# w_down by products over all rows, from block sums that are made earlier and stored

## The chip, the cores and the metric

The kernel runs on one core of one Trainium2 chip. The metric is the device time in microseconds (us) of one execution. The core has five engines that run side by side: PE (TensorE, matmuls), DVE (VectorE), ACT (ScalarE), POOL (GpSimd) and SP (SyncE, which here issues nearly all DMA transfers). Each works through its own queue in order, and an instruction waits at the head of its queue until what it needs is done.

## The reference, cut to what matters

A decoder layer in float32 for 1024 positions and a width of 1024:

```python
h = rmsnorm(x, norm_mix)
proj = h @ w_in
y_a = (g_s5 @ w_a_val) * sigmoid(g_s5 @ w_a_gate)      # g_s5 = gelu(S5 state-space mixer)
y_b = mamba2_mixer(...) @ w_b
y_c = memory_attention(...) @ w_c
x = x + (g_a * y_a + g_b * y_b + g_c * y_c) @ w_out
h = rmsnorm(x, norm_ffn)
up = causal_dwconv(h @ w_up)                           # 2 x 2816 channels, width 3
x = x + (silu(up[..., :2816]) * up[..., 2816:]) @ w_down
return rmsnorm(x, norm_final)
```

The change touches the last product (2816 rows of w_down), the places where its operands come into being, and one buffer of the S5 mixer.

## The kernel before, in words

**Matmuls in float32.** `split_into` (line 140) splits each operand into a high part (a copy on ACT into fp32r) and a low part (a subtraction on DVE, or on POOL where `e=G`). `mm3` (346) then makes three matmuls: high x high, high x low, low x high. All elementwise two-operand work goes through `tt` (125), and the recorder of line 51 stands for every instruction in the profile, so the profile names tiles rather than lines.

**Weights.** `w_raw` (240) loads weights into a ring of 3 raw buffers (`wr`), `w_ent` (261) splits them into a ring of 6 entries (`wh`, `wl`), and `take` (291) hands them out, up to 6 entries ahead of use. All loads are issued by SP.

**The tag ev.** Many short-lived tiles share a ring of 4 buffers in the pool `ep`, tag `ev`. In the S5 stage these are the outputs of the gate products (`qt`, `gt`), the loaded parameters `s5bc`, the decay `s5D0` and the temporary `s5ph` of the phases.

**The S5 stage** (`s5_work`, 773) runs as a generator beside the gate products: after every quarter of a product's matmuls (`tick`, 330) it may take a step. ACT and PE keep the program's order there. It works on four quarters of the channels. For each, `double` (896) makes 128 phases on POOL by seven doublings (`cmul`, 624, six operations each); PE transposes the input maps (`s5bps`), ACT copies them out (`s5BTr`, `s5BTi`); `lag_maps` (865) makes the lag map, to which POOL adds the diagonal (`s5w`) before it is stored in `kS` and loaded back; `scan` (924) and `back` (942) on DVE make the states `s5Hr`, `s5Hi`; `outputs` (957) multiplies them on PE (`s5yp`).

**w_a, w_b.** `gemm_fm` (354) makes 48 matmuls for one block of 128 columns over all 1024 positions. Eight pairs of products of w_a (gate, value) are followed by 16 of w_b. `y_norm` (1477) runs beside them: it loads the 16 blocks of y (`yq`, 2 buffers), squares them on ACT, adds them on POOL and makes the reciprocal norm. `load_chunk` (1426) loads and splits the moving operands (`ck`, `hl`) between w_a and w_b.

**w_up.** Blocks of 128 channels; the first 3 pairs (activation, gate) by plain products, the others by `wino_run` (395): seven products for a pair of blocks instead of eight, a Strassen-Winograd scheme, 84 matmuls for a pair. POOL makes the sums of the weights' blocks (`wS`). The epilogue `ff_epi` makes the convolution (`ff_conv`, two operations on DVE), the silu on ACT, and `ff_b` (1608) the gated product on DVE, which it stores in DRAM as `aS`, one row block of 128 channels at a time.

**w_down, before.** The same scheme of seven products (`PRODS`, 219) for out = A B, with A the activations and B = w_down, cut in half by rows (blocks k and k + 11), by positions and by columns. It runs over three chunks of 4, 4 and 3 row blocks (`CUT`, 221): for each chunk all seven products, P1, P2, P6, P5, P7, P3, P4. `d_load` (1656) loads whole rows of 512 KB for a chunk; `d_prep` (1673) splits the operands of one entry (a product's block of rows), and, at the entries of P2, P6 and P5, makes the sums S1 to S4 (DVE) and T1 to T4 (POOL) in place. Some splits are given to POOL. An entry feeds 12 matmuls; 77 entries in all. After each product and chunk `done` (1774) adds the accumulators `dP` into the rows `x1f` (first by an ACT copy); the residual rows are loaded from `x1S` and added on POOL during the second chunk. `half_done` (1734) and `final_norm` (1741) make the last norm: blocks 0 to 3 after the last P3, blocks 4 to 7 at the end of the last P4, whose 3 entries are run block by block.

The first four entries are prepared before the epilogue of the last pair of w_up (`ff_last`), in the order in which ACT must take them. From `SY.on = True` (1717) on, SP issues transfers in the program's order.

Of the kernel before, what the change touches and what calls it, by code (L numbers as in the profile page):

```python
# [58 lines left out]
def hybrid_layer(ctx: ExitStack, tc: tile.TileContext, a: dict, out: bass.AP):  # L59
# [161 lines left out]
    CUT, NK = [0, 4, 8, 11], NFF // 2  # L221
    NC = len(CUT) - 1
    D_POOL = {"S1", "S2", "S3", "S4"}
    prods = [(p, c) for c in range(NC) for p in ("P1", "P2", "P6", "P5", "P7", "P3", "P4")]
    dents = [(p, c, k) for p, c in prods for k in range(CUT[c], CUT[c + 1])]
# [392 lines left out]
    aS = dram("aS", [DFF, T])  # L618
# [858 lines left out]
    def y_norm():  # L1477

        acc = wbp.tile([P, T], F32, name="acc")
        for i in range(16):  # L1480
            yq = wbp.tile([P, T], F32, tag="yq", name="yq", bufs=2)
            SY.dma_start(out=yq, in_=ySSD[i * P:(i + 1) * P, :])
            S.activation(out=acc if i == 0 else yq, in_=yq, func=AF.Square)
            if i:
                tt(acc, acc, yq, ALU.add, G)
            yield
        sst = ps.tile([P, 8], F32, tag="s", name="sst")
        for i in range(8):
            TE.matmul(sst[:, i:i + 1], acc[:, i * P:(i + 1) * P], ones[:, 0:1], start=True, stop=True)
        ivt = wbp.tile([P, 8], F32, name="ivt")  # L1490
        rsqrt(ivt, sst, 8, 1.0 / 2048, cp)
        yield
        for hf in range(2):
            ib = ps.tile([P, 4, P], F32, tag="s", name="ib")
            for i in range(4):
                dgi = wbp.tile([P, P], F32, tag="dgi", name="dgi", bufs=4)
# [29 lines left out]
    for pr in range(2):  # L1526
# [62 lines left out]
    ff = ExitStack()  # L1589
    t3p = ff.enter_context(pool("t3p", side="right"))  # L1590
# [16 lines left out]

    def ff_b(j, va, ob):
        vb = ff_conv(NFF + j, ob)
        tt(va, va, vb, ALU.mult)  # L1610
        SY.dma_start(out=aS[j * P:(j + 1) * P, :], in_=va)

    def ff_epi(n, ua, ub):
        ff_b(FF_PLAIN + n, ff_a(FF_PLAIN + n, ua), ub)
# [31 lines left out]

    set_banks("5", 0, 8)
    dap = ctx.enter_context(pool("da"))
    dps = [ctx.enter_context(pool(nm, side="right")) for nm in ("dw1", "dw2", "da1", "da2")]
    dxp = ctx.enter_context(pool("dx", side="right"))  # L1650
    xfp = ctx.enter_context(pool("xf", side="right"))
    lo, hi = slice(0, HALF), slice(HALF, T)
    blk, dready = {}, deque()
    dpos = {"ent": 0, "use": 0}

    def d_load(k, b, halves=False):

        kk = k + NK * b
        rw = dps[b].tile([P, T], F32, tag="r", name=f"rw{b}", bufs=4)
        ra = dps[2 + b].tile([P, T], F32, tag="r", name=f"ra{b}", bufs=4)  # L1660
        names = (("A12", "A22"), ("B21", "B22")) if b else (("A11", "A21"), ("B11", "B12"))
        srcs = (aS[kk * P:(kk + 1) * P, :], a["w_down"][0][kk * P:(kk + 1) * P, :])
        parts = []
        for t, nms, src in zip((ra, rw), names, srcs):
            for s, nm in zip((lo, hi), nms):
                blk[nm, k] = t[:, s]
            if halves:
                parts.append([(t[:, s], src[:, s]) for s in (lo, hi)])
            else:
                SY.dma_start(out=t, in_=src)  # L1670
        return parts

    def d_prep():

        p, c, k = dents[dpos["ent"]]
        dpos["ent"] += 1
        an, wn_ = PRODS[p]
        r = []
        for nm, pl, tg, bufs in ((an, dap, "a", RING), (wn_, wp, "w", RING)):
            h = pl.tile([P, HALF], F32R, tag=tg + "h", name=tg + "h", bufs=bufs)  # L1680
            l = pl.tile([P, HALF], F32R, tag=tg + "l", name=tg + "l", bufs=bufs)
# [4 lines left out]
        def new(s, nm):  # L1686
            blk[nm, k] = dxp.tile([P, HALF], F32, tag=s, name=s, bufs=4)
            return blk[nm, k]

        def inplace(nm, old, i0, i1, e=V):  # L1690
            o = blk[old, k]
            tt(o, blk[i0, k], blk[i1, k], ALU.subtract, e)
            blk[nm, k] = o

        if p == "P2":
            tt(new("xa", "S1"), blk["A21", k], blk["A22", k], ALU.add)
            tt(new("xw", "T1"), blk["B12", k], blk["B11", k], ALU.subtract, G)
            inplace("S3", "A21", "A11", "A21")
            inplace("S2", "A11", "S1", "A11")
            inplace("T2", "B11", "B22", "T1", G)  # L1700
            inplace("S4", "A12", "A12", "S2")
        elif p == "P6":
            inplace("T3", "B12", "B22", "B12", G)
        elif p == "P5":
            inplace("T4", "B21", "B21", "T2", G)
        elif p in ("P7", "P4") and c + 1 < NC:
            kn = k - CUT[c] + CUT[c + 1]
            if kn < CUT[c + 2]:
                d_load(kn, int(p == "P4"))
# [8 lines left out]
    first = [(d_load(k, 0, True), d_load(k, 1, True)) for k in range(CUT[1])]
    for parts in [f[0] for f in first] + [f[1] for f in first]:
        for t in parts:  # L1720
            SY.dma_start(out=t[0][0], in_=t[0][1])
# [35 lines left out]
    FIRST = {("P1", 0), ("P6", 0), ("P5", 0), ("P7", 0)}  # L1757
    acc4 = [None, None]
    TE.on = True
    for p, c in prods:  # L1760
        n = CUT[c + 1] - CUT[c]
        last = (p, c) == prods[-1]
        more = p in ("P6", "P7", "P3")
        tg = (prods.index((p, c))) % 2
        if not more:
            acc4[tg] = [ps2[tg].tile([P, HALF], F32, tag="s", name=f"d{p}") for _ in range(4)]
        bank = acc4[tg]

        def part(i, k, r):
            ah, al, bh, bl = r  # L1770
            mm3(bank[i], [(ah[:, i * P:(i + 1) * P], al[:, i * P:(i + 1) * P], bh, bl)],
                first=k == 0 and not more, last=k == n - 1, again=more)

        def done(i):
            for q, (i0, s) in enumerate(DST[p]):
                xc = x1[i0 + i][:, s]
                if (p, c) in FIRST and q == 0:
                    copy(xc, bank[i])
                else:
                    tt(xc, xc, bank[i], ALU.add)  # L1780
# [11 lines left out]
        for k in range(n):  # L1792
            r = d_take()
            for i in range(4):
                part(i, k, r)
        for i in range(4):
            done(i)
        if c == 1 and p in ("P1", "P6", "P7", "P4"):
            for i in range(2):
                i += 2 * ("P1", "P6", "P7", "P4").index(p)  # L1800
                xr = ep.tile([P, D], F32, tag="ev", name="x1r", bufs=4)
                SY.dma_start(out=xr, in_=x1S[i * P:(i + 1) * P, :])
                tt(x1[i], x1[i], xr, ALU.add, G)
        if c == NC - 1:
            for i in range(4):
                if p in ("P2", "P7", "P3"):
                    half_done(i + 4 * (p == "P7"), lo if p == "P2" else hi)
            if p == "P3":
                final_norm(0, 4)
# [25 lines left out]
```

## Time and profile before

| | us |
|---|---|
| median of 3 runs | 2365.66 (2365.19 to 2370.77) |
| the profiled execution, its own time | 2366.27 |
| its span from the first to the last instruction | 2364.6 |
| PE, busy (modelled) | 2215.3 (94%) |
| PE, weight loads | 1833.3 (78%) |
| DVE, busy | 1697.1 (72%) |
| ACT, busy | 987.4 (42%) |
| POOL, busy | 912.3 (39%) |
| stage of S5 beside the gates, about | 522 to 800 |
| w_a and w_b | 1218 to 1562 |
| w_up | 1671 to 2098 |
| w_down and the last norm | 2098 to 2364.6 |

Matmuls overlap, so a matmul of 389 ns is followed by the next after less than that; the pace is read from the distance of starts. In a group of instructions, "idle before" is the time the engine stood idle just before them, with what ended it. A wait names whose event ended it, not necessarily the cause behind that.

### The profile page before, as it was taken

How to read it: one execution, taken by the hardware profiler on the slowest of the kernel's cores; microseconds unless marked ns; L12 is line 12 of the kernel's file. 1: busy time of each engine (PE TensorE's matmuls, PEld its weight loads, DVE VectorE, ACT ScalarE, POOL GpSimd, SP SyncE). 2: the span in 40 equal slices, each digit the busy share in tenths (PEclk: the TensorE clock that was granted, in tenths of full speed). 3: DMA queues.
4: the chain of work that ended last, by engine and by line, in shares of the span. 5: the costliest groups of instructions: out<-in, count | busy, mean ns of one | idle time of the engine just before them, and what ended most of it. 6: DMA issues, size and time to landing. Idle time of an engine off the chain costs nothing. (4 is left out here: it accounts for less than half of the span.)

```text
span 2364.6 us, 30701 instructions
## 1 busy us (share of the span) xinstructions
PE 2215.3 (94%) x11239; PEld 1833.3 (78%) x11239; DVE 1697.1 (72%) x2320; ACT 987.4 (42%) x1762; POOL 912.3 (39%) x691
## 2 busy tenths in 40 slices
PE   6999999998878999999989999999999999987996
PEld 5777888887667788777768888899788888876775
DVE  7899877876556576989463264534977787878998
ACT  4435545542222366565351132122355455444434
POOL 4422433426566005888140002200323333353775
PEclk9999999999999999999999999999999999998998
DMA  4323434465344447997762254432122222243231
GB/s 146 108 81 98 125 107 125 125 147 106 74 94 102 126 131 247 301 293 256 250 230 71 73 169 135 132 116 90 63 80 83 87 81 81 72 175 125 82 118 71
DMA packets 339191, 305.95 MB, mean 129 GB/s; under 512 B 31969, under 2 KB 297057, under 8 KB 339041
## 3 DMA queue, kind: packets, MB, share of 16 engines
q1 hardware_dynamic: 337888, 299.80, 41.3%
q10 hardware_dynamic: 1152, 4.19, 0.4%
q8 instruction: 88, 1.44, 0.2%
q14 instruction: 63, 0.51, 0.1%
HBM read 226.61 MB, written 77.33 MB: 129 GB/s over the span
## 5 line engine op out<-in xcount | busy, mean ns | idle before, releaser
L51 DVE TENSOR_TENSOR wl<-wr,wh 128x512 fp32r<-128x512 f32 (+1 forms) x275 | 223.6, 824 | 170.2 <-ACT wh L51 163.9
L51 ACT ACTIVATE wh<-wr 128x512 fp32r<-128x512 f32 (+1 forms) x305 | 186.6, 625 | 374.5 <-PE g L51 224.6
L51 PE MATMUL g<-hlH,wh 128*128 128x512 f32 x736 | 288.8, 394 | 8.6 <-DVE fv L51 4.6
L51 PE MATMUL g<-hlL,wh 128*128 128x512 f32 x736 | 289.7, 394 | 5.5 <-DVE hlL L51 5.5
L51 PE MATMUL g<-hlH,wl 128*128 128x512 f32 x736 | 288.2, 392 | 0.0
L51 POOL TENSOR_TENSOR wS<-wr 128x512 f32<-128x512 f32 x82 | 128.2, 1563 | 346.5 <-DMA wr<-in_w_in 155.7
L51 PE MATMUL gh<-hlH,wh 128*128 128x512 f32 (+1 forms) x464 | 193.7, 418 | 0.0
L51 PE MATMUL gh<-hlH,wl 128*128 128x512 f32 (+1 forms) x464 | 183.0, 394 | 0.0
L51 PE MATMUL gh<-hlL,wh 128*128 128x512 f32 (+1 forms) x464 | 182.8, 394 | 0.0
L51 DVE TENSOR_TENSOR wl<-wS,wh 128x512 fp32r<-128x512 f32 x164 | 129.8, 793 | 70.4 <-ACT wh L51 70.3
L51 PEld LDWEIGHTS g<-hlH,wh 128*128 128x128 f32 x736 | 139.4, 189 | 39.3 <-issue 5.4
L51 PEld LDWEIGHTS g<-hlL,wh 128*128 128x128 f32 x736 | 139.2, 189 | 38.6 <-DVE hlL L51 10.4
L51 ACT ACTIVATE wh<-wS 128x512 fp32r<-128x512 f32 x164 | 102.4, 628 | 148.4 <-PE wA L51 90.5
L51 PEld LDWEIGHTS g<-hlH,wl 128*128 128x128 f32 x736 | 139.2, 189 | 28.4
L51 POOL TENSOR_TENSOR wS<-wr,wS 128x512 f32<-128x512 f32 x41 | 94.8, 2313 | 153.7 <-DVE wl L51 143.8
L51 POOL TENSOR_TENSOR mg<-mg,gi 128x1024 f32<-128x1024 f32 x15 | 41.8, 2784 | 275.5 <-DVE gi L51 275.5
L51 PE MATMUL dP<-wh,ah 128*128 128x512 f32 x308 | 122.6, 398 | 14.9 <-ACT ah L51 9.0
L51 PE MATMUL dP<-wl,ah 128*128 128x512 f32 x308 | 122.6, 398 | 12.6 <-DVE wl L51 12.6
L51 PE MATMUL dP<-wh,al 128*128 128x512 f32 x308 | 121.9, 396 | 1.8 <-POOL al L51 1.8
L51 PEld LDWEIGHTS gh<-hlH,wh 128*128 128x128 f32 (+1 forms) x464 | 87.4, 188 | 24.2 <-issue 5.4
L51 PEld LDWEIGHTS gh<-hlL,wh 128*128 128x128 f32 (+1 forms) x464 | 87.3, 188 | 21.8 <-issue 3.6
L51 PEld LDWEIGHTS gh<-hlH,wl 128*128 128x128 f32 (+1 forms) x464 | 86.9, 187 | 20.8
(389 smaller groups left out, 6078.3 us busy)
## 6 DMA issues: line engine op xcount, KB each, us to landing
wr<-in_w_in SPq DMA_DIRECT2D x76, 512.0 KB, 3.7
wr<-in_w_up SPq DMA_DIRECT2D x44, 512.0 KB, 3.7
xc<-xcS SPq DMA_DIRECT2D x32, 640.0 KB, 5.8
seg<-aD SPq DMA_DIRECT2D x32, 512.0 KB, 7.0
gi<-gS SPq DMA_DIRECT2D x32, 512.0 KB, 3.8
xcS<-xv SPq DMA_DIRECT2D x24, 512.0 KB
gS<-gt SPq DMA_DIRECT2D x24, 512.0 KB, 4.4
aS<-fv SPq DMA_DIRECT2D x22, 512.0 KB, 2.6
```

The costliest lines, as they stand in the source:

```text
L51: r = f(*args, **kw)
```

## The change

Four things change together.

1. The row blocks are paired as 2k and 2k + 1 (not k and k + 11), and the seven products run one after the other over all 11 pairs, with no chunks.
2. All block sums are made earlier and stored in DRAM. `down_sums` makes T1 to T4 of w_down on POOL, in 22 pieces of 128 x (2 x 256), in steps beside w_a and the first eight products of w_b, and stores them in `tS`. `ff_sums` makes S1 to S4 on DVE when the second block of a pair is finished in w_up, and stores all seven operands in `aS`. For the last pair it runs within P1 of w_down.
3. In w_down, `d_raw` loads one 256 KB block of each operand per entry, 4 entries ahead of the splits; all splits are on ACT and DVE, none on POOL. x1 is loaded whole from `x1S` within P1 and every accumulator is added to it on DVE.
4. In S5, `double` takes its temporary from the stage's own pool (tag `ph`) and writes the first product of each component directly in place.

Along with this, `yq` has 1 buffer (2 before), `dgi` 2 (4 before), and the steps of `y_norm` are taken one per product.

The diff, cut to its core:

```diff
-    CUT, NK = [0, 4, 8, 11], NFF // 2
+    NK = NFF // 2
+    A_AT = {n: i for i, n in enumerate(("A11", "S3", "A12", "A22", "S2", "S4", "S1"))}
+    T_AT = {n: i for i, n in enumerate(("T1", "T2", "T3", "T4"))}
+    dents = [(p, k) for p in PRODS for k in range(NK)]
...
-    aS = dram("aS", [DFF, T])
+    aS = dram("aS", [NK, P, 7, HALF])
+    tS = dram("tS", [NK, P, 4, HALF])
...
             def double(R, jj, ks):
                 Rr, Ri = R
-                tmp = ep.tile([P, 2, 8, 64], F32, tag="ev", name="s5ph", bufs=4)
                 for k in ks:
                     n = 1 << k
-                    cmul(Rr[:, :, n:2 * n], Ri[:, :, n:2 * n], bc(er[:, k, jj], n), bc(ei[:, k, jj], n),
-                         Rr[:, :, 0:n], Ri[:, :, 0:n], tmp[:, 0, :, 0:n], tmp[:, 1, :, 0:n], G)
+                    tmp = sp.tile([P, 8, 64], F32, tag="ph", name="s5ph")[:, :, 0:n]
+                    e_r, e_i = bc(er[:, k, jj], n), bc(ei[:, k, jj], n)
+                    r0, i0, r1, i1 = Rr[:, :, 0:n], Ri[:, :, 0:n], Rr[:, :, n:2 * n], Ri[:, :, n:2 * n]
+                    tt(r1, e_r, r0, ALU.mult, G)
+                    tt(tmp, e_i, i0, ALU.mult, G)
+                    tt(r1, r1, tmp, ALU.subtract, G)
+                    tt(i1, e_r, i0, ALU.mult, G)
+                    tt(tmp, e_i, r0, ALU.mult, G)
+                    tt(i1, i1, tmp, ALU.add, G)
...
+    def down_sums():
+        pieces = [(k, c) for k in range(NK) for c in range(2)]
+        got = {}
+        for n in range(len(pieces) + 2):
+            if n >= 2:
+                (k, c), (r0, r1, t) = pieces[n - 2], got.pop(n - 2)
+                cs = slice(c * 256, (c + 1) * 256)
+                SY.dma_start(out=tS[k, :, 0:2, cs], in_=t)
+                SY.dma_start(out=tS[k, :, 2, cs], in_=r0[:, 1, :])
+                SY.dma_start(out=tS[k, :, 3, cs], in_=r1[:, 0, :])
+            if n < len(pieces):
+                k, c = pieces[n]
+                rs = []
+                for b in range(2):
+                    r = wbp.tile([P, 2, 256], F32, tag=f"dr{b}", name=f"dr{b}", bufs=2)
+                    rows = a["w_down"][0][(2 * k + b) * P:(2 * k + b + 1) * P]
+                    SY.dma_start(out=r, in_=rows.rearrange("p (h x) -> p h x", h=2)[:, :, c * 256:(c + 1) * 256])
+                    rs.append(r)
+                got[n] = rs
+            if 1 <= n <= len(pieces):
+                r0, r1 = got[n - 1]
+                t = wbp.tile([P, 2, 256], F32, tag="dt", name="dt")
+                tt(t[:, 0, :], r0[:, 1, :], r0[:, 0, :], ALU.subtract, G)
+                tt(r0[:, 1, :], r1[:, 1, :], r0[:, 1, :], ALU.subtract, G)
+                tt(t[:, 1, :], r1[:, 1, :], t[:, 0, :], ALU.subtract, G)
+                tt(r1[:, 0, :], r1[:, 0, :], t[:, 1, :], ALU.subtract, G)
+                got[n - 1] = r0, r1, t
+            yield
...
         og = gemm_fm(("p", "w_a_gate", 0, KD, m * P, P), mv_c(cg), m == 0)
-        for _ in range(2 if m < 6 else 1):
-            next(yn, None)
+        next(yn, None)
+        next(dn, None)
...
         ov = gemm_fm(("p", "w_a_val", 0, KD, m * P, P), mv_c(cg))
+        next(yn, None)
+        next(dn, None)
...
             o = gemm_fm(("p", "w_b", pr * 1024, KD, m * P, P), mv_c(cy), m == 0)
+            next(dn, None)
...
+    def ff_sums(kp, h, v, w, s1):
+        tt(s1, h[:, hi], v[:, hi], ALU.add)
+        tt(w[:, lo], s1, h[:, lo], ALU.subtract)
+        tt(h[:, hi], h[:, lo], h[:, hi], ALU.subtract)
+        tt(w[:, hi], v[:, lo], w[:, lo], ALU.subtract)
+        for n, t in enumerate((h, v, w)):
+            SY.dma_start(out=aS[kp, :, 2 * n:2 * n + 2, :], in_=t.rearrange("p (h x) -> p h x", h=2))
+        SY.dma_start(out=aS[kp, :, 6, :], in_=s1)
...
     def ff_b(j, va, ob):
         vb = ff_conv(NFF + j, ob)
-        tt(va, va, vb, ALU.mult)
-        SY.dma_start(out=aS[j * P:(j + 1) * P, :], in_=va)
+        kp, odd = divmod(j, 2)
+        if odd:
+            tt(va, va, vb, ALU.mult)
+            if kp in held:
+                ff_sums(kp, held.pop(kp), va, vb, fsp.tile([P, HALF], F32, tag="fs1", name="fs1", bufs=2))
+            else:
+                return va, vb
+        elif kp < NK - 1:
+            held[kp] = fsp.tile([P, T], F32, tag="fh", name="fh")
+            tt(held[kp], va, vb, ALU.mult)
+        else:
+            tt(va, va, vb, ALU.mult)
+            SY.dma_start(out=aS[kp, :, 0:2, :], in_=va.rearrange("p (h x) -> p h x", h=2))
...
+    def d_raw():
+        p, k = dents[dpos["raw"]]
+        dpos["raw"] += 1
+        an, wn_ = PRODS[p]
+        if wn_ in T_AT:
+            ws = tS[k, :, T_AT[wn_], :]
+        else:
+            r = 2 * k + (wn_ != "B11")
+            ws = a["w_down"][0][r * P:(r + 1) * P, hi if wn_ == "B22" else lo]
+        r = []
+        for tg, src in (("ra", aS[k, :, A_AT[an], :]), ("rw", ws)):
+            t = drp.tile([P, HALF], F32, tag=tg, name=tg, bufs=DRAWS)
+            SY.dma_start(out=t, in_=src)
+            r.append(t)
+        draw.append(r)
...
-            split_into(h, l, blk[nm, k], e=G if (nm in D_POOL if c else p == "P1" or nm == "A12" and k > 1) else V)
+            split_into(h, l, raw_)
...
     def d_take(live=0):
         while dpos["ent"] < min(dpos["use"] - live + RING, len(dents)):
+            if not draw:
+                d_raw()
             d_prep()
+            while dpos["raw"] < min(dpos["ent"] + DRAWS, len(dents)):
+                d_raw()
...
-    for _ in first:
+    for _ in range(DRAWS):
         d_prep()
-    ff_epi(*ff_last[0])
+    va = xfp.tile([P, T], F32, name="fh20")
+    SY.dma_start(out=va.rearrange("p (h x) -> p h x", h=2), in_=aS[NK - 1, :, 0:2, :])
+    vs = ff_epi(*ff_last[0])
...
+        tail = 3 if last else 0
+        for k in range(NK - tail):
+            r = d_take()
+            for i in range(4):
+                part(i, k, r)
+            if n == 0 and k == 2:
+                for i in range(8):
+                    SY.dma_start(out=x1[i], in_=x1S[i * P:(i + 1) * P, :])
+            if n == 0 and k == 5:
+                ff_sums(NK - 1, va, *vs, xfp.tile([P, HALF], F32, name="fs20"))
+                gain_row(a["norm_final"], gfin)
```

More of the change, by code (lines that the diff above doesn't have):

```diff
@@ L1480, in y_norm @@
         for i in range(16):
-            yq = wbp.tile([P, T], F32, tag="yq", name="yq", bufs=2)
+            yq = wbp.tile([P, T], F32, tag="yq", name="yq")
             SY.dma_start(out=yq, in_=ySSD[i * P:(i + 1) * P, :])
@@ L1495, in y_norm @@
             for i in range(4):
-                dgi = wbp.tile([P, P], F32, tag="dgi", name="dgi", bufs=4)
+                dgi = wbp.tile([P, P], F32, tag="dgi", name="dgi", bufs=2)
                 ts(dgi, ident, ivt[:, hf * 4 + i:hf * 4 + i + 1], ALU.mult)
@@ L1648, in hybrid_layer @@
     dap = ctx.enter_context(pool("da"))
-    dps = [ctx.enter_context(pool(nm, side="right")) for nm in ("dw1", "dw2", "da1", "da2")]
-    dxp = ctx.enter_context(pool("dx", side="right"))
+    drp = ctx.enter_context(pool("dr"))
     xfp = ctx.enter_context(pool("xf", side="right"))
[L1652 to L1671, printed above, removed]
+    draw, dready = deque(), deque()
@@ new lines, in hybrid_layer @@
+    dpos = {"raw": 0, "ent": 0, "use": 0}
+    def d_raw():
[13 more added lines that the diff above has]
+        draw.append(r)
@@ L1683, in d_prep @@
             r += [h, l]
         dready.append(r)
[L1686 to L1709, printed above, removed]
@@ L1711, in d_take @@
     def d_take(live=0):
         while dpos["ent"] < min(dpos["use"] - live + RING, len(dents)):
+            if not draw:
+                d_raw()
             d_prep()
+            while dpos["raw"] < min(dpos["ent"] + DRAWS, len(dents)):
+                d_raw()
         dpos["use"] += 1
         return dready.popleft()
+    DRAWS = 4
     SY.on = True
[L1718 to L1721, printed above, removed]
@@ L1722, in hybrid_layer @@
-    for f in first:
-        for t in f[0] + f[1]:
-            SY.dma_start(out=t[1][0], in_=t[1][1])
+    for _ in range(DRAWS):
+        d_raw()
     S.on, S.prev = True, None
-    for _ in first:
+    for _ in range(DRAWS):
         d_prep()
-    ff_epi(*ff_last[0])
+    va = xfp.tile([P, T], F32, name="fh20")
+    SY.dma_start(out=va.rearrange("p (h x) -> p h x", h=2), in_=aS[NK - 1, :, 0:2, :])
+    vs = ff_epi(*ff_last[0])
     S.on = False
-    gfin = gain_row(a["norm_final"], xfp)
     x1 = [xfp.tile([P, D], F32, name=f"x1f{i}") for i in range(8)]
+    gfin = xfp.tile([P, D], F32, name="gfin")
@@ L1756, in hybrid_layer @@
            "P7": ((4, lo), (4, hi)), "P3": ((0, hi),), "P4": ((4, lo),)}
-    FIRST = {("P1", 0), ("P6", 0), ("P5", 0), ("P7", 0)}
     acc4 = [None, None]
     TE.on = True
-    for p, c in prods:
-        n = CUT[c + 1] - CUT[c]
-        last = (p, c) == prods[-1]
+    for n, p in enumerate(PRODS):
+        last = n == len(PRODS) - 1
         more = p in ("P6", "P7", "P3")
-        tg = (prods.index((p, c))) % 2
         if not more:
-            acc4[tg] = [ps2[tg].tile([P, HALF], F32, tag="s", name=f"d{p}") for _ in range(4)]
-        bank = acc4[tg]
+            acc4[n % 2] = [ps2[n % 2].tile([P, HALF], F32, tag="s", name=f"d{p}") for _ in range(4)]
+        bank = acc4[n % 2]
         def part(i, k, r):
@@ L1771, in part @@
             mm3(bank[i], [(ah[:, i * P:(i + 1) * P], al[:, i * P:(i + 1) * P], bh, bl)],
-                first=k == 0 and not more, last=k == n - 1, again=more)
+                first=k == 0 and not more, last=k == NK - 1, again=more)
         def done(i):
-            for q, (i0, s) in enumerate(DST[p]):
+            for i0, s in DST[p]:
                 xc = x1[i0 + i][:, s]
[L1777 to L1780, printed above, removed]
+                tt(xc, xc, bank[i], ALU.add)
+        tail = 3 if last else 0
[9 more added lines that the diff above has]
+                gain_row(a["norm_final"], gfin)
         if last:
-            rs_ = [d_take(k) for k in range(n)]
+            rs_ = [d_take(k) for k in range(tail)]
             for i in range(4):
-                for k in range(n):
-                    part(i, k, rs_[k])
+                for k in range(tail):
+                    part(i, NK - tail + k, rs_[k])
                 done(i)
@@ L1791, in hybrid_layer @@
             break
[L1792 to L1795, printed above, removed]
         for i in range(4):
             done(i)
[L1798 to L1809, printed above, removed]
+        for i in range(4):
+            if p in ("P2", "P7", "P3"):
+                half_done(i + 4 * (p == "P7"), lo if p == "P2" else hi)
+        if p == "P3":
+            final_norm(0, 4)
 _INS = ["x", "mem", "norm_mix", "w_in", "s5_lambda_re", "s5_lambda_im", "s5_log_dt", "s5_b_re", "s5_b_im",
```

19 lines of the change are left out of this document (8 added, 11 removed).

## Prediction

> **What bounds the kernel now.** I read the page first: PE is busy 94% of the span, so time can only come out of the places where PE idles or runs at the half clock. The waits of PE, by stretch, say where these are. First the stretch of the w_down products (columns: who waited for whom, us in total, times, longest):
>
> ```profile
> PE dP L51 <- DVE wl L51: 12.6, 2, 12.2
> PE dP L51 <- ACT ah L51: 9.0, 1, 9.0
> PE dP L51 <- DVE x1f L51: 5.9, 2, 3.1
> PE dP L51 <- POOL al L51: 1.8, 1, 1.8
> ```
>
> 29.3 us of waits. The instructions of the accumulators dP (first and last start behind the durations) and the pitch of twelve matmuls in the chain that ended last:
>
> ```profile
> L51 PE MATMUL dP<-wh,ah x308: 388/389/793, 2098.3 to 2344.0; 128*128 128x512 f32 x154
> L51 PE MATMUL dP<-wh,al x308: 387/389/628, 2098.7 to 2344.4; 128*128 128x512 f32 x154
> 2084.86 2.72 PE wC L51 x12
> ```
>
> The 3 x 308 = 924 matmuls need 924 x 2.72 / 12 = 209.4 us at full clock; they stand from 2098.3 to 2344.8, 246.5 us. So 37.1 us are lost, 29.3 in waits and 7.8 in slow restarts. The stretches (PE, PEld, DVE, ACT, POOL busy, granted clock, DMA share, GB/s) and the timeline say why:
>
> ```profile
> 2098.00:2143.00 45.00, 23.54 (x100) 18.08 (x98) 42.08 (x30) 17.63 (x29) 40.62 (x24) 0.80 0.48 170
> 2131.01 1.74 DVE L51 TENSOR_TENSOR ra<-ra,ra 128x512 f32<-128x512 f32 x1
> 2132.16 1.70 POOL L51 TENSOR_TENSOR xw<-rw 128x512 f32<-128x512 f32 x1
> 2144.17 0.68 DVE L51 TENSOR_TENSOR ra<-ra,ra 128x512 f32<-128x512 f32 x1
> ```
>
> In the first 45 us DVE and POOL are both full with block sums and splits, and the same DVE subtraction takes 1.74 us beside POOL and 0.68 us without it. PE starves on both.
>
> The second place is the S5 stage; PE's largest wait from 500 to 800, and what ACT waits for there (two windows):
>
> ```profile
> PE s5bps L51 <- ACT s5BTr L51: 29.4, 3, 12.1
> ACT qt L51 <- POOL s5Ri L51: 12.7, 1, 12.7
> ACT gt L51 <- POOL s5Ri L51: 23.1, 2, 12.6
> ```
>
> ACT's eviction of a gate product wants a buffer of the tag ev that the phase temporary s5ph still holds; the copies s5BTr stand behind it in ACT's queue, and PE behind those.
>
> **The change part by part.**
>
> *w_down products: gain 33 us.* Matmuls stay 924. Every sum and every split by POOL leaves the stage, and a product runs over all 11 rows, so an entry is two ACT copies and two DVE splits per 12 matmuls. Of before (count, busy, mean ns, idle before):
>
> ```profile
> L51 ACT ACTIVATE ah<-ra 128x512 fp32r<-128x512 f32 x64 | 40.3, 630 | 104.9 <-PE dP L51 64.7 <-DVE ra L51 37.1 <-issue 3.1
> L51 DVE TENSOR_TENSOR x1f<-x1f,dP 128x512 f32<-128x512 f32 x80 | 50.1, 676 | 1.3 <-PE dP L51 1.3
> ```
>
> DVE: 154 splits x 0.68 + 32 additions x 0.676 = 126 us of 209; ACT: 154 x 0.63 = 97. Neither binds. At the start the last pair's epilogue is still on DVE (one of its operations over 128x1024, and an issue on SP, for later):
>
> ```profile
> 1872.19 1.27 DVE L51 SCALAR_TENSOR_TENSOR fv<-ua,colsC,fv 128x1022 f32<-128x1022 f32 x1
> 597.13 0.38 SPq L51 DMA_DIRECT2D wr<-in_w_in  x1
> ```
>
> Two additions (1.4), four fv and the product at 1.27 (6.4) and the next four splits (2.7) are 10.4 us, while PE lives 10.9 us on the four entries prepared ahead: it just fits. The load fh20, put into SP's queue behind the first four pairs of loads, waits for memory that the last w_up products release; the loads of entry 4 stand behind it and have the same 10.9 us. ff_sums of the last rows comes five entries later, in DVE time that is then spare. I keep 4 us of residual loss (bounds 0 and 12): 246.5 - 213.4 = 33.
>
> The new loads are 154 of 256 KB, 40.4 MB: 193 GB/s over 209 us, beside the 4.2 MB of x1 in one burst. Rows of before (KB, us to landing; then a stretch with its rate):
>
> ```profile
> rw<-in_w_down SPq DMA_DIRECT2D x16, 256.0 KB, 5.5
> x1r<-x1S SPq DMA_DIRECT2D x8, 512.0 KB, 8.2
> 960.00:1080.00 120.00, 117.63 (x803) 93.63 (x802) 105.83 (x130) 72.36 (x191) 99.50 (x64) 1.00 0.91 297
> ```
>
> The kernel has moved 297 GB/s, and loads are issued four entries (10.9 us) before the split that needs them; the slowest row lands in 8.2. Hidden, with 2.7 us to spare. SP issues two per 2.72 us, at 0.38 each. The Trainium skill (DMA: Bandwidth & Descriptors, the measured table under Bandwidth) speaks against this part: it wants transfers of 1 MiB or more for three quarters of the peak and gives 138 GB/s at 64 KB and 341 at 1 MB. An estimate at its lower figure is 40.4 MB / 138 GB/s = 293 us for the products, and a sum of 2392 in place of 2312; the trace does not agree as far as it goes, with its 297 GB/s from transfers of 640 KB and less.
>
> *Tail: gain 5 us.* The first and the last of the four additions into x1 behind the last product:
>
> ```profile
> 2343.41 0.68 DVE L51 TENSOR_TENSOR x1f<-x1f,dP 128x512 f32<-128x512 f32 x1
> 2353.07 0.68 DVE L51 TENSOR_TENSOR x1f<-x1f,dP 128x512 f32<-128x512 f32 x1
> ```
>
> The fourth starts 8.3 us after PE's end (2344.8), since DVE is still at the norm of blocks 0 to 3, which P3 released only three entries (8 us) before. Now P4 has 11 entries, 30 us, for that. The norm of blocks 4 and 5 can still come ahead of the last additions, so I take 5 of the 8.3 (bounds 0 and 7).
>
> *S5 phases: gain 22 us.* Same POOL operations, but s5ph leaves the ring ev. So ACT's wait and with it PE's three waits go. What is late next is the chain of the S5 itself, once around for one quarter of the channels:
>
> ```profile
> 609.09 1.12 PE L51 MATMUL s5bps<-ident,s5BAi 128*128 128x128 f32 x4 [10.47 <-ACT s5BTr L51]
> 609.86 0.78 PE L51 MATMUL gh<-hlH,wh 128*128 128x512 f32 x1
> 612.57 0.58 PE L51 MATMUL gh<-hlH,wh 128*128 128x512 f32 x1
> 614.93 1.29 POOL L51 TENSOR_TENSOR s5Ri<-s5ph 128x512 f32<-128x512 f32 x1
> 625.24 0.31 POOL L51 TENSOR_TENSOR s5w<-s5w,s5dg 32x64 f32<-32x64 f32 x1
> 629.99 0.69 DVE L51 TENSOR_TENSOR s5w<-s5si,s5Ri 128x512 f32<-128x512 f32 x1 [6.15 <-DMA kS<-s5w]
> 640.37 0.68 DVE L51 SCALAR_TENSOR_TENSOR s5Hi<-s5Hi,s5w 128x508 f32<-128x508 f32 x1
> 642.05 0.60 PE L51 MATMUL s5yp<-s5U,s5T 128*128 128x128 f32 x4
> ```
>
> PE would come 10.5 us earlier, and 1.3 more without the slow restart (six matmuls from 609.86 to 612.57 in 2.71 us, for 1.36). But its s5yp at 642.05 reads what DVE finishes at 641.05, only 1.0 us before. DVE's scan waits for the stored lag map, that for POOL's addition at 625.24, and POOL is through with the phases at 616.2: the addition can move up by 9.0 us, not by 11.8. So about 9 per quarter for the two long waits and what is left (6.8 + 1.3) for the third: 26, less some for POOL's s5bd copies, which lie inside the doubling and now face an earlier PE: 22. Bounds: 8, if POOL's order keeps the additions late, and 33, all waits and restarts.
>
> *Sums of w_down beside w_a and w_b: loss 5 us.* 22 pieces, each 2 loads, 3 stores and 4 POOL subtractions of 128x256:
>
> ```profile
> L51 POOL TENSOR_TENSOR s5Rr<-s5ph 128x256 f32<-128x256 f32 x4 | 2.9, 719 | 0.3
> L51 POOL TENSOR_TENSOR rw<-rw,rw 128x512 f32<-128x512 f32 x22 | 36.6, 1668 | 28.5 <-DMA rw<-in_w_down 13.4 <-DVE wl L51 12.1 <-DVE ra L51 1.9
> ```
>
> 88 x 0.72 = 63 us, or 73 at half of the longer row. The stage:
>
> ```profile
> 1218.00:1387.00 169.00, 168.76 (x760) 139.78 (x759) 58.93 (x76) 36.27 (x49) 13.03 (x5) 1.00 0.30 94
> 1387.00:1397.00 10.00, 9.50 (x42) 7.23 (x40) 7.63 (x8) 5.04 (x6) 0.00 (x0) 1.00 0.83 290
> 1397.00:1563.00 166.00, 166.00 (x736) 137.34 (x736) 83.93 (x83) 36.34 (x54) 41.76 (x15) 1.00 0.40 125
> ```
>
> POOL comes to 55 + 73 = 128 of 345 us. DVE has 150; even if each POOL us became one DVE us it would have 223. So the bulk hides. SP is in order: the load of a piece waits for the store of the piece two before, which the same step has just issued. Behind it stand weights, gates and chunks of y:
>
> ```profile
> aS<-fv SPq DMA_DIRECT2D x22, 512.0 KB, 2.6
> ySSD<-y SPq DMA_DIRECT2D x32, 256.0 KB, 4.7
> SPq L51 <- DVE wl L51: 205.8, 29, 11.5
> ```
>
> A step holds SP for 2.6 to 4.7 us and 5 issues of 0.4: under 7 of the 10.9 us of a product (48 matmuls). SP already waits up to 11.5 us for a free weight buffer without PE feeling it. Only the change from w_a to w_b (1387 to 1397) is just in time, at 290 GB/s: there one step's 1.05 MB costs 3.6 us and a store's landing a few more. 5 us; bounds 0 and 12. Fewer buffers for yq and dgi: nothing, half a product now lies between two steps.
>
> *Sums of the gated activations: loss 1 us.* Four DVE operations of 128x512 per pair of row blocks, one pair of blocks in 38.1 us (two times seven times 2.72):
>
> ```profile
> 1741.00:2090.00 349.00, 349.00 (x1542) 288.97 (x1541) 270.47 (x292) 173.54 (x253) 113.95 (x68) 1.00 0.24 79
> ```
>
> DVE has 29.5 us in 38.1; with 4 x 0.68 it is 32.2, with all four beside POOL at 1.74 it is 36.5. Below 38.1 both ways, and weights are six entries ahead. Their stores on SP (four where there were two) wait for DVE, and weight loads wait behind them by as much; the ring covers that too. 1 us; bounds 0 and 6.
>
> **Sum.** 33 + 5 + 22 - 5 - 1 = 54 us. The profiled execution took 2366.27 (span 2364.6), 0.6 above the median of the runs: 2366.3 - 54 = 2312.3, in terms of the median 2311.7, so 2312. All best bounds together (37 + 7 + 33) give 2289, all worst (25 + 0 + 8 - 12 - 6 = 15) 2351.
>
> **The rivals.** *The S5 chain keeps its pace.* Another tile of the ring ev, or POOL's order, takes the place of s5ph, and only 8 us or fewer come out: about 2328. For it: the 1.0 us margin at 642.05. Against: both rows of ACT's wait name s5Ri and nothing else.
>
> *SP detention makes it slower.* Place: the 24 steps of the new sums. The sum without its 5 us there gains 59; if each step stalled PE by more than 59 / 24 = 2.5 us, it is slower than before. At 3.5 us: 84 - 59, so 2391. For it: SP is in order and 205.8 us of its time there are waits. Against: weights are asked for three raw buffers and six entries ahead.
>
> *The load stream binds the products.* It decides where landing passes 10.9 us; at 16 us (twice the slowest row) an entry takes 16 / 4 = 4.0 us, 77 x 4.0 = 308 against 213: 2407. The Trainium skill's rule on small transfers (DMA: Bandwidth & Descriptors, Bandwidth) points this way. For it: twice as many loads of half the size, and x1 in a burst. Against: 8.2 us and 297 GB/s.
>
> *Nothing moves:* the start of the products still starves, with waits for loads in place of the sums that left it, and the S5 gives its lower bound: 8 - 5 - 1 = 2, so 2364.
>
> **Chances.** My sum 0.72; slower S5 chain 0.15; SP 0.05; load stream 0.04; nothing moves 0.04. A measurement of this kernel can tell about 0.3%, 7 us. Faster 0.89, same 0.04, slower 0.07. The range reaches from near the best bounds, 2290, over the slower chain to 2340; outside it lie the three last cases and the tail of all worst bounds.
>
> **What would show it.** Right: PE's wait for s5BTr gone; dP within 217 us from first to last start, POOL idle in it and no DVE split at 1.7; last x1f addition within 4 us of the last matmul. Wrong: s5bps or s5yp waiting for DVE or POOL by 5 us or more per quarter; PE waits on g of more than 12 us from 1218 to 1563; dP waiting for ACT ah behind DMA ra.

## The result, and the profile after

| | before | after |
|---|---|---|
| median of 4 runs, us | 2365.43 (2363.95 to 2370.77) | 2325.96 (2323.82 to 2329.99) |
| span of the profiled execution, us | 2364.6 | 2323.1 |
| granted clock, mean over the span | 0.977 | 0.984 |

The ratio is 0.9834, with a 95% interval of 0.9822 to 0.9846: 1.7% faster, 39.5 us between the medians and 41.5 us between the two profiled spans. The forecast was 2312, so 14 us of the forecast gain of 54 did not come. The spans can be cut at fixed places of the program to see which 14.

**The products of w_down.** The accumulators dP by tile (durations, then first and last start), and the one wait of PE that is left there:

```profile
L51 PE MATMUL dP<-wh,ah x308: 388/389/494, 2098.9 to 2308.7; 128*128 128x512 f32 x154
L51 PE MATMUL dP<-wh,al x308: 388/389/398, 2099.4 to 2309.2; 128*128 128x512 f32 x154
```

```profile
PE dP L51 <- DVE wl L51: 0.2, 1, 0.2
```

From 2098.9 to 2309.6 are 210.7 us, where it took 246.5: 35.8 gained. The 924 matmuls need 209.4, so 1.3 us of loss are left of 37.1. The first stretch of the products, and the group of DVE's splits of the activations:

```profile
2099.00:2144.00 45.00, 44.63 (x196) 36.43 (x195) 30.70 (x47) 20.91 (x34) 0.00 (x0) 1.00 0.90 327
```

```profile
L51 DVE TENSOR_TENSOR al<-ra,ah 128x512 fp32r<-128x512 f32 x77 | 56.3, 731 | 66.9 <-ACT ah L51 66.8
```

POOL (the fifth busy time) stands still in this stretch, and PE (the first) is busy 44.6 of 45 us in place of 23.5. Over the whole stage a split takes 0.73 us on the mean. DMA moved 327 GB/s in the stretch. Later POOL isn't as idle as the prediction's sign had it: it makes the 16 multiplications of the last norm (23.0 us), and four splits beside them take 1.77 or 1.78 us.

**The tail.** The additions of the accumulators into x1:

```profile
L51 DVE TENSOR_TENSOR x1f<-x1f,dP x32: 679/682/690, 2127.0 to 2311.9; 128x512 f32<-128x512 f32 x32
```

The last starts 2.3 us behind the last matmul, where it was 8.3; from the last matmul to the end it is 13.5 us in place of 19.8: 6.3 gained.

**The S5 stage and what follows it.** The last gate product of the kernel (tile gh) and the first of w_out (tile wops), first of the kernel before and then of the changed one:

```profile
L51 PE MATMUL gh<-hlH,wh x464: 387/389/799, 522.9 to 1151.1; 128*128 128x512 f32 x150, 128*32 128x512 f32 x5
L51 PE MATMUL wops<-wh,hlH x256: 277/283/385, 1561.9 to 1658.2; 128*128 128x256 f32 x128
```

```profile
L51 PE MATMUL gh<-hlH,wh x464: 387/389/799, 522.9 to 1147.6; 128*128 128x512 f32 x150, 128*32 128x512 f32 x5
L51 PE MATMUL wops<-wh,hlH x256: 277/283/388, 1562.5 to 1658.8; 128*128 128x256 f32 x128
```

All of the S5 lies before the last gh, and that came only 3.5 us earlier. From there to the first wops it is 414.9 us in place of 410.8, so w_a and w_b lost 4.1. From the last wops to the first dP it is 440.1 in both, so the sums of the gated activations cost nothing. 35.8 + 6.3 + 3.5 - 4.1 is 41.5, the whole difference of the spans. Only one term is far off: the S5 phases, 3.5 in place of 22. PE's waits there, of the changed kernel from 500 to 800:

```profile
PE s5kps L51 <- POOL s5bd L51: 31.0, 7, 13.7
PE s5sr L51 <- DVE s5Y L51: 3.6, 1, 3.6
PE s5bps L51 <- DVE s5BAi L51: 1.2, 1, 1.2
```

The wait for s5BTr, 29.4 us before, is gone as forecast. In its place stands a wait for s5bd, which was 4.4 in the kernel before:

```profile
PE s5kps L51 <- POOL s5bd L51: 4.4, 1, 4.4
```

The timeline of the second quarter shows why; first the kernel before (POOL, then PE), then the changed one:

```profile
607.86 0.64 POOL L51 COPY s5bd<-s5BAr 64x128 f32<-64x128 f32 x2
608.59 0.66 POOL L51 TENSOR_SCALAR s5bd<-s5BAi 64x128 f32<-64x128 f32 x2
609.32 1.04 POOL L51 TENSOR_TENSOR s5ph<-s5keep,s5Rr 128x512 f32<-128x512 f32 x1
617.45 0.38 PE L51 MATMUL s5kps<-s5CAr,s5bd 128*32 128x128 f32 x2 [0.45 <-DVE s5CAr L51]
```

```profile
612.93 2.24 POOL L51 TENSOR_TENSOR s5Rr<-s5Rr,s5ph 128x512 f32<-128x512 f32 x1
615.12 1.63 POOL L51 COPY s5bd<-s5BAr 64x128 f32<-64x128 f32 x2
616.83 1.04 POOL L51 TENSOR_TENSOR s5ph<-s5keep,s5Rr 128x512 f32<-128x512 f32 x1
619.18 0.67 POOL L51 TENSOR_SCALAR s5bd<-s5BAi 64x128 f32<-64x128 f32 x2
616.80 0.64 PE L51 MATMUL s5kps<-s5CAr,s5bd 128*32 128x128 f32 x2 [4.86 <-POOL s5bd L51]
619.90 0.64 PE L51 MATMUL s5kps<-s5CAi,s5bd 128*32 128x128 f32 x2 [2.46 <-POOL s5bd L51]
```

Before, the four small copies into s5bd stood ahead of the last doubling (its 128x512 operations start at 609.32). In the changed kernel the doublings stand earlier in POOL's queue, and the copies have come to stand within and behind the last of them. PE arrived earlier and waited for them instead. Both kernels name the copies before the doublings in their source, so this order was made when the programs were built, and the traces show only its outcome. That the temporary, which no longer waits for the ring ev, is what moved it is inferred; no run separates it from the first products that are now written in place.

### The profile page after: what moved, and what is told of

Read it like the earlier page. It is cut to its first block, busy times and chain, and to the rows that moved or that the text cites. A ratio compares the mean times of both kernels' runs of the same rounds, so it can differ in the third digit from the quotient of the medians.

```text
span 2323.1 us, 31155 instructions
## 1 busy us (share of the span) xinstructions
PE 2210.0 (95%) x11239; PEld 1828.8 (79%) x11239; DVE 1649.3 (71%) x2310; ACT 981.4 (42%) x1746; POOL 857.6 (37%) x689
## 5 line engine op out<-in xcount | busy, mean ns | idle before, releaser
L51 DVE TENSOR_TENSOR wl<-wr,wh 128x512 fp32r<-128x512 f32 (+1 forms) x275 | 233.4, 859 | 168.6 <-ACT wh L51 167.0
L51 DVE TENSOR_TENSOR wl<-wS,wh 128x512 fp32r<-128x512 f32 x164 | 135.5, 831 | 36.6 <-ACT wh L51 36.4
L51 POOL TENSOR_TENSOR x1f<-x1f,gfin 128x512 f32<-128x512 f32 x16 | 23.0, 1459 | 224.3 <-ACT sq L51 224.3
L51 DVE TENSOR_TENSOR al<-ra,ah 128x512 fp32r<-128x512 f32 x77 | 56.3, 731 | 66.9 <-ACT ah L51 66.8
```

Of the source, the lines that this page charges most:

```text
L51: r = f(*args, **kw)
```

## The experiments

The theory: the S5 part lost its gain to POOL's own queue, in which the copies into s5bd stand behind the doublings. The rivals: another part of the change took the gain back, or the S5's own chain (scan, lag map, POOL's additions) can't go faster. All runs are compared with the kernel before, on the same chip.

**s5_only: the S5 part alone**

```diff
 (the kernel before)
-                tmp = ep.tile([P, 2, 8, 64], F32, tag="ev", name="s5ph", bufs=4)
+                    tmp = sp.tile([P, 8, 64], F32, tag="ph", name="s5ph")[:, :, 0:n]
... (and the six operations in place of cmul, as in the change)
```

> The kernel before with one part of the change alone: the phase temporaries of the S5 stage in a buffer of their own. Theory (POOL's queue: the four copies into s5bd now stand between or behind the doublings, and the matmuls into s5kps wait for them): the S5 stage gives only the 3.5 us that the last gate matmul of after came earlier, so about 2362, with PE's wait s5kps <- POOL s5bd near 31 us and no wait for s5BTr. Rival (the part is worth the 22 us of the prediction, and another part of the change took it back): about 2344, with s5kps waiting less than 10 us.

Measured: 2364.14 us, ratio 0.9989 (0.9981 to 0.9998), a gain of about 2 us (1.8 between the medians, 2.6 by the ratio). Its wait:

```profile
PE s5kps L51 <- POOL s5bd L51: 31.2, 7, 13.8
```

The part alone gives as little as within the whole change, with the same new wait. The rival that something else took it back falls.

**without_s5: the change without its S5 part**

```diff
 (the changed kernel)
-                    tmp = sp.tile([P, 8, 64], F32, tag="ph", name="s5ph")[:, :, 0:n]
+                tmp = ep.tile([P, 2, 8, 64], F32, tag="ev", name="s5ph", bufs=4)
... (and cmul in place of the six operations)
```

> The changed kernel with the S5 part alone undone. If the parts add up as their stretches say, 2 to 4 us more than the changed kernel: 2328 to 2330, with PE's wait for s5BTr near 29 us. If the part is worth more beside the other parts than alone: 2335 or more.

Measured: 2329.99 us, ratio 0.9848 (0.9831 to 0.9864); PE waits 28.6 us for s5BTr. Its interval overlaps that of the changed kernel. The part is worth about 2 to 4 us either way: 1.8 to 2.6 when it is put in alone, 3.3 to 4.0 when it is taken out alone.

**bd_dve: the copies into s5bd on DVE**

```diff
 (the changed kernel)
-                    G.tensor_copy(bd[pp, 0, :, g2, :], BAr[pp, :, 7, :])
-                    G.tensor_scalar(out=bd[pp, 1, :, g2, :], in0=BAi[pp, :, 7, :], scalar1=-1.0,
+                    V.tensor_copy(bd[pp, 0, :, g2, :], BAr[pp, :, 7, :])
+                    V.tensor_scalar(out=bd[pp, 1, :, g2, :], in0=BAi[pp, :, 7, :], scalar1=-1.0,
```

> The changed kernel with the 16 small copies into s5bd (64x8x16 each, four per quarter) on DVE in place of POOL, right behind the DVE operations that make their inputs; nothing else moves. Theory (POOL's queue is what the S5 stage lost): PE's wait s5kps <- POOL s5bd of 31 us goes, and 15 to 22 us come out, so 2304 to 2311. Rival (the S5's own chain keeps its pace: scan, stored lag map and POOL's additions): the wait turns into one for s5yp or s5sr on DVE or POOL, and 8 us or less come out: 2318 or more.

Measured: 2313.61 us, ratio 0.9784 (0.9771 to 0.9798). The wait for s5bd is gone; 12 us came out, between the two expectations. What stands in the way now (PE's waits, 500 to 800):

```profile
PE s5sr L51 <- DVE s5Y L51: 11.6, 1, 11.6
PE s5kps L51 <- DVE s5CAr L51: 7.1, 4, 1.9
PE s5kps L51 <- DVE s5CAi L51: 4.7, 4, 1.3
```

The 11.6 us are one event of the fourth quarter. Followed back in the timeline, engine by engine:

```profile
735.70 1.97 PE L51 MATMUL s5sr<-s5U,s5BTr 128*64 128x128 f32 x16 [11.56 <-DVE s5Y L51]
733.57 0.69 DVE L51 SCALAR_TENSOR_TENSOR s5Y<-s5Y,s5yp 128x512 f32<-128x512 f32 x1 [14.91 <-ACT s5Y L51]
732.94 0.60 ACT L51 ACTIVATE s5Y<-s5yp 128x512 f32<-128x512 f32 x1 [22.05 <-DMA yS<-s5Y]
695.15 0.33 SPq L51 DMA_DIRECT2D gS<-gt  x1
726.72 0.38 SPq L51 DMA_DIRECT2D wr<-in_w_in  x1
727.19 3.89 SPq L51 DMA_DIRECT2D yS<-s5Y  x8
724.21 2.48 POOL L51 TENSOR_TENSOR wl<-wr,wh 128x512 fp32r<-128x512 f32 x2
```

PE waits for DVE, DVE for ACT, ACT for the store of the s5Y before; that store stands on SP behind a weight load, SP issues nothing from 695.5 to 726.7, and the load goes out when POOL has split the weights whose buffer it takes. That split stands in POOL's queue behind the doublings. So the queue of POOL was still the cause, four engines away from PE.

**bd_act: the same copies on ACT**

```diff
 (the changed kernel)
-                    G.tensor_copy(bd[pp, 0, :, g2, :], BAr[pp, :, 7, :])
-                    G.tensor_scalar(out=bd[pp, 1, :, g2, :], in0=BAi[pp, :, 7, :], scalar1=-1.0,
-                                    scalar2=0.0, op0=ALU.mult, op1=ALU.add)
+                    copy(bd[pp, 0, :, g2, :], BAr[pp, :, 7, :])
+                    copy(bd[pp, 1, :, g2, :], BAi[pp, :, 7, :], -1.0)
```

> The changed kernel with the same 16 copies into s5bd on ACT, which is the least loaded engine of the stage but runs in order behind the evictions of the gate products. Theory (any engine whose queue is not behind the doublings does): as with DVE, 2304 to 2313; if only the copies by DVE help, because ACT's copies stand behind an eviction, 2316 or more and a wait of PE for ACT s5bd. Rival (own chain): 2318 or more on both engines.

Measured: 2339.75 us, ratio 0.9892 (0.9878 to 0.9905), 14 us slower than the changed kernel. ACT's own waits and timeline:

```profile
ACT s5bd L51 <- DVE s5BAr L51: 59.1, 3, 20.1
```

```profile
568.61 0.60 ACT L51 ACTIVATE qt<-gh 128x512 f32<-128x512 f32 x1 [3.85 <-issue]
589.35 0.31 ACT L51 ACTIVATE s5bd<-s5BAr 64x128 f32<-64x128 f32 x1 [20.13 <-DVE s5BAr L51]
```

Slower, but for another reason than either expectation named: not that the copies stood behind evictions, but that evictions stood behind the copies. ACT keeps the program's order here and reaches the copies 20 us before DVE has their input; behind them wait the evictions of the gate products. PE's longest wait becomes s5sr, 20.2 us in three.

**bd_dve_nopool: the weight splits off POOL too**

```diff
 (bd_dve)
-    on_pool = {win(C_U), win(C_U + P)} | {win(C_Q + m * P) for m in range(4)} | {win(C_G + m * P) for m in G_S5}
+    on_pool = {win(C_U), win(C_U + P)}
```

> bd_dve, and the low parts (wl) of the 26 weight splits of the query and gate products of the S5 stage on DVE in place of POOL, where they stand behind the doublings. Theory (POOL's queue still costs there: a weight load on SP waits for a buffer that the split on POOL frees, the store of s5Y stands behind that load, ACT waits 22 us for the store and PE 11.6 us in s5sr): the wait of 11.6 goes, 6 to 12 us less than bd_dve, 2302 to 2308. Rival (DVE makes the S5's own chain, and 26 x 0.68 = 18 us more on it cost more than the queue): 2314 to 2330, with more of PE's waits on DVE.

Measured: 2299.19 us, ratio 0.9722 (0.9705 to 0.9739), 14 us below bd_dve, somewhat more than the theory gave. PE's waits and the stretch of the S5:

```profile
PE s5kps L51 <- DVE s5CAr L51: 7.4, 4, 2.6
PE s5kps L51 <- DVE s5CAi L51: 6.4, 4, 1.6
PE s5bps L51 <- DVE s5BAi L51: 1.9, 1, 1.9
```

```profile
500.00:800.00 300.00, 284.19 (x1757) 232.62 (x1757) 220.48 (x313) 92.14 (x165) 126.37 (x199) 0.98 0.50 114
```

The same stretch of the changed kernel:

```profile
500.00:800.00 300.00, 263.97 (x1603) 213.71 (x1602) 184.81 (x240) 80.72 (x144) 161.47 (x241) 0.94 0.47 104
```

The s5sr wait is gone. DVE is busy 220 of 300 us in place of 185, and the granted clock is 0.98 in place of 0.94. This version beats both kernels: 2.8% below before, and about 1.1% below the change (0.9722 / 0.9834 = 0.9886; the two intervals lie apart). It does the same operations, 42 of them on another engine.

**splits_alone and own_undone: one part of that version taken out**

```diff
 splits_alone (bd_dve_nopool)
-                    V.tensor_copy(bd[pp, 0, :, g2, :], BAr[pp, :, 7, :])
-                    V.tensor_scalar(out=bd[pp, 1, :, g2, :], in0=BAi[pp, :, 7, :], scalar1=-1.0,
+                    G.tensor_copy(bd[pp, 0, :, g2, :], BAr[pp, :, 7, :])
+                    G.tensor_scalar(out=bd[pp, 1, :, g2, :], in0=BAi[pp, :, 7, :], scalar1=-1.0,
 own_undone (bd_dve_nopool)
-                    tmp = sp.tile([P, 8, 64], F32, tag="ph", name="s5ph")[:, :, 0:n]
+                tmp = ep.tile([P, 2, 8, 64], F32, tag="ev", name="s5ph", bufs=4)
... (and cmul in place of the six operations)
```

> The changed kernel with the 26 low parts of the weights of the query and gate products on DVE, and the copies into s5bd left on POOL. Theory (the copies stand behind the doublings, whatever else POOL has): the wait s5kps <- POOL s5bd stays at 20 us or more, and 2309 to 2318 come out, near bd_dve. Rival (POOL was only too full: 37 us less on it bring the copies forward in time): 2299 to 2303, as bd_dve_nopool.

> bd_dve_nopool with the S5 part of the change undone: the phase temporaries are again in the ring ev, four times two buffers. Theory (the buffer of its own is worth what the prediction gave it, 22 us, once nothing else stands in POOL's queue): the wait of PE for s5BTr comes back and 15 us or more are lost, 2314 or more. Rival (POOL's queue was all that the stage lost, and the ring ev came free too late only because POOL was late): 2299 to 2304.

splits_alone took 2318.24 us, ratio 0.9805 (0.9790 to 0.9821), at the upper end of the theory; the copies still run behind the doublings (first and last at 553.9 and 734.6). Only the first quarter's 10.5 us of PE's wait carry the name s5bd; 16.5 us in the other three are put down to ACT's s5Y. In the second quarter PE starts at 615.74, ACT's s5Y ended at 615.73 and the first copies at 615.68, so there the profile doesn't say which of the two PE waited for. The two moves help each other: by the ratios the copies alone are worth 12 us, the splits alone 7, and both together 26.

own_undone took 2315.17 us, ratio 0.9789 (0.9774 to 0.9804), and the old wait is back:

```profile
PE s5bps L51 <- ACT s5BTr L51: 23.9, 3, 8.9
```

So the buffer of its own, worth 2 to 4 us in the change as it is, is worth 16 us where POOL's queue is clear of what PE and SP wait for. Of the prediction's 22 us, 16 are there once the next waits in line are gone too; those waits are what it left out.

**bd_dve_small: the other small operations too**

```diff
 (bd_dve)
-                    tt(KT[:, :, 0:16], KT[:, :, 0:16], dg, ALU.add, G)
+                    tt(KT[:, :, 0:16], KT[:, :, 0:16], dg, ALU.add)
-                G.memset(D0[:, :, 0:1], 0.0)
+                V.memset(D0[:, :, 0:1], 0.0)
```

> bd_dve, and the other small operations of the S5 that stand behind the doublings on POOL (the clearing of one column of s5D, and the addition into the stored lag map, 12 in all) on DVE. Theory (the queue of POOL is only felt where PE waits for it): the addition comes 2 to 3 us earlier per quarter, and since nothing of PE waits for it in bd_dve, 0 to 4 us: 2310 to 2314. Rival (each small operation behind the doublings costs as the copies into s5bd did, about 3 us per quarter): 2300 to 2304.

Measured: 2317.28 us, ratio 0.9794 (0.9779 to 0.9810), within the interval of bd_dve: no gain, and a miss by 3 us of the theory's upper end. PE did not wait for these operations, so moving them buys nothing. The rival's 2300 is excluded.

**no_sums: w_a and w_b without the sums of w_down**

```diff
 (the changed kernel; down_sums only yields)
-            ws = tS[k, :, T_AT[wn_], :]
+            r, h = divmod(T_AT[wn_], 2)
+            ws = a["w_down"][0][(2 * k + r) * P:(2 * k + r + 1) * P, (lo, hi)[h]]
```

> The changed kernel without the sums of blocks of w_down: no loads, no POOL subtractions and no stores beside w_a and w_b, and the products P6, P5, P7 and P4 read a plain block of w_down in place of T2, T1, T3 and T4 (the output is left wrong by that). Theory: these sums are what the stretch of w_a and w_b lost, so 4 us less than the changed kernel: 2322, with the stretch from the last gate matmul to the first of w_out at about 411 us in place of 415. Rival (the loss comes from what else moved there: the half clock behind the change of chunks, and the two buffers in place of four for dgi): within 1 us, 2325 to 2327.

Measured: 2323.28 us, ratio 0.9818 (0.9804 to 0.9831). The interval overlaps that of the changed kernel, so the time alone does not settle it. The stretch from the last gh to the first wops leaves out the S5. It is 410.8 us before, 410.9 in s5_only and 412.3 here, all without these sums; it is 414.9 in the changed kernel, and in the ten profiled kernels with the sums 412.6 to 418.3, on the mean 414.7. Against this run the sums cost 2.6 us in the changed kernel and 2.4 on the mean; the ten scatter by more than that. The 1.5 us by which this run is longer than the kernel before are not theirs. One wait goes with the sums:

```profile
PE ib L51 <- DVE dgi L51: 1.9, 1, 1.9
```

It stands in all ten kernels with them (0.8 to 3.9 us) and in none of the three without.

**pool_split: splits of the activations on POOL in w_down**

```diff
 (the changed kernel)
-            split_into(h, l, raw_)
+            split_into(h, l, raw_, e=G if tg == "a" else V)
```

> The changed kernel with the low parts (al) of the 77 activation blocks of the w_down products on POOL in place of DVE; no sums are there. Theory (the sums filled DVE and POOL at the start, and that starved PE; a split on each of the two engines per 2.72 us does not): DVE at 0.7 to 1.7 us and POOL at 1.3 to 1.8 us per entry both stay below 2.72, so dP within 214 us and 2325 to 2330. Rival (DVE and POOL side by side are what cost, with or without sums): waits of dP for POOL al or DVE wl of 10 us and more, 2337 or more.

Measured: 2328.61 us, ratio 0.9843 (0.9827 to 0.9859); dP takes 214.5 us (2097.3 to 2311.8), 3.8 more than in the changed kernel, of which 3.3 are waits. The two groups that now run side by side:

```profile
L51 POOL TENSOR_TENSOR al<-ra,ah 128x512 fp32r<-128x512 f32 x77 | 112.4, 1471 | 108.1 <-ACT ah L51 107.9
L51 DVE TENSOR_TENSOR wl<-rw,wh 128x512 fp32r<-128x512 f32 x77 | 101.3, 1330 | 69.7 <-ACT wh L51 69.6
```

DVE's split goes from 0.72 to 1.33 us, and still both stay below the 2.72 us that PE needs for an entry. So a split on each engine costs little beside the 37.1 us that were lost before. That the sums starved the products is argued, not shown, since no run puts them back. The profile before speaks for it: in its first 45 us they took 20.8 of the 42.1 busy us of DVE and 28.6 of the 40.6 of POOL.

**loads_two: half the buffers of the loads**

```diff
 (the changed kernel)
-    DRAWS = 4
+    DRAWS = 2
```

> The changed kernel with two buffers for each kind of raw block of the w_down products in place of four, so two entries of loads in flight. Theory (the loads are hidden by their lead, which must exceed landing, issue and split): an entry takes (landing + 1.7) / 2; with the landing of 5.2 us that stands in the changed kernel that is 3.45 us against 2.72, 56 us more, 2382; if landing falls to 3.5 us with fewer in flight it is 2.6, and nothing is lost. Rival (six prepared entries cover the loads whatever their lead): 2324 to 2328 with landing above 3.8 us.

The edit does one thing more than this says: the loop that prepares entries ahead of the last epilogue of w_up counts to DRAWS too, so two entries are prepared there in place of four.

Measured: 2344.55 us, ratio 0.9908 (0.9894 to 0.9922), about 18 us slower than the changed kernel (dP takes 228.4 us in place of 210.7); neither figure of the theory. PE's longest wait in the products; then ACT's at the burst of x1, here and in the changed kernel (there with SP's issues around it):

```profile
PE dP L51 <- ACT wh L51: 11.3, 4, 6.7
```

```profile
2134.89 0.63 ACT L51 ACTIVATE ah<-ra 128x512 fp32r<-128x512 f32 x1 [10.27 <-DMA ra<-aS]
```

```profile
2112.56 4.93 SPq L51 DMA_DIRECT2D x1f<-x1S  x8
2118.50 0.32 SPq L51 DMA_DIRECT2D ra<-aS  x1
2128.10 0.63 ACT L51 ACTIVATE ah<-ra 128x512 fp32r<-128x512 f32 x1 [11.75 <-DMA ra<-aS]
```

With two in flight the median landing of ra falls to 3.3 us (5.2 with four), and from 2200 to 2260 PE has no gap, so the steady state holds, as the second half of the theory had it. But the ring of prepared entries is no longer full when the burst of x1 takes SP for 4.6 us and the DMA behind it: ten entries are ready and PE is in the ninth, where the changed kernel has twelve ready and is in the eighth. ACT then waits 10.3 us, and PE 6.7. Behind the stores of the last sums ACT waits again, 7.7 us, and PE 2.7. In the changed kernel ACT waits 11.75 us at the burst and PE nothing: its twelve entries last until 2131.5, and the next is ready at 2130.2. Four buffers and four entries prepared ahead hide the burst, with about 1 us to spare; which of the two halves lost the 18 us, this run does not separate.

## Why the prediction was right or wrong

- **w_down products, 33 us: right.** 35.8 by the span of dP. The residual loss of 4 us was 1.3. The waits for ACT and DVE went together with the sums; that they went because of them is argued (pool_split). The loads are hidden with four buffers and not with two (loads_two). The case against the part from the Trainium skill (DMA: Bandwidth & Descriptors, the rule on batching under Bandwidth) does not hold here: transfers of 256 and 512 KB, several in flight, moved 327 GB/s in the first 45 us.
- **Tail, 5 us: right**, 6.3.
- **S5 phases, 22 us: the step that failed**, with 3.5. The term was "26, less some for POOL's s5bd copies, which lie inside the doubling and now face an earlier PE". The mechanism named for the gain was the right one: the wait for s5BTr went, and it came back with the part undone (own_undone). But the "some" was put at 4 us and PE waited 31. The working moved the start of PE forward and left POOL's order as it stood in the profile of before. With the part in, the doublings stand ahead of the copies in POOL's queue, so the copies became later (615.12 in place of 607.86) while PE became earlier. Its lower bound, 8, "if POOL's order keeps the additions late", looked at the wrong operations of that queue, the additions, and was still too high. The rival of a slower S5 chain named POOL's order too, and its 2328 is nearest to what was measured; the run of bd_dve_nopool shows that the chain itself was not the limit. The signs of being wrong missed the place too: they named s5bps and s5yp, and the wait was in s5kps.
- **Sums of w_down, 5 us lost: right in size**, 4.1 by the profile, of which no_sums gives 2.6 to the sums. The place was named only in part. It was to be the issue on SP at the change from w_a to w_b. Matched by the starts of their matmuls, the changed kernel falls behind the kernel before by 1.6 us at the change from w_c to w_a, by 2.2 at the matmuls of y_norm that wait for dgi, and by 1.0 at the change from w_a to w_b, and 0.7 come back ahead of w_out. The wait for dgi isn't due to its fewer buffers alone, since no_sums has the same two and no such wait. What makes the rest was not settled.
- **Sums of the gated activations, 1 us lost: right**, nothing measurable.
- **The sum.** 54 forecast, 41.5 by the spans. The S5 fell 18.5 short and the other terms gave 6 more than asked, so 12.5 are missing. That the errors have opposite signs is luck; that the time lies in the range is not, since its upper end was drawn over the slower S5.

## What to carry to other kernels

When a resource is freed on an engine that works in order, look at what the freed instructions now stand in front of: list that queue's small operations for which other engines wait, and price each at the whole length of the work that may move ahead of it. When a long wait is taken out of PE, expect the next one at the same place, follow it back engine by engine, and judge the first part only once the second is out: the buffer was worth about 3 us before and 16 us after. Here the small copies did best on the engine that makes their input (2313.6 us) and worst on the one that was least busy (2339.8).

## What was not expected of the hardware

A tiny operation on POOL was held for as long as DVE had two-operand work back to back. In the changed kernel DVE works from 584.67 to 595.1 without a gap (the first and the last of twelve operations are shown). POOL's operation over 128x8 takes 8.42 us there, and the next of its kind 0.21:

```profile
584.67 0.66 DVE L51 TENSOR_TENSOR s5Hr<-s5W,s5Rr 128x508 f32<-128x508 f32 x1
593.92 1.22 DVE L51 TENSOR_TENSOR s5BAi<-s5BAi,s5w 128x1024 f32<-128x1024 f32 x1
586.79 8.42 POOL L51 TENSOR_TENSOR s5ph<-s5keep,s5Ri 128x8 f32<-128x8 f32 x1
595.17 0.21 POOL L51 TENSOR_TENSOR s5Ri<-s5keep,s5Ri 128x8 f32<-128x8 f32 x1
```

The held operation is the first of the quarter's doublings, so all of them start later by it; the third and the fourth quarter show it too, with 8.43 us each.

The Trainium skill (SBUF — State Buffer, SBUF: two separate sides) says of the port pair that DVE and GpSimd share that it is an exclusive lock, and that the loser blocks for the whole instruction. The rows agree, and show more: here the loser stayed blocked over a whole train of instructions.
